# Products first, into all four accumulators: the order of work inside a seven-product matrix multiplication

## The chip, the core and the metric

The kernel runs on one core of one Trainium2 chip. The metric is device time in microseconds (us) of one execution, lower is better. TensorE is called PE below, VectorE DVE, ScalarE ACT, GpSimd POOL and the queue of SyncE SP, as in the profile.

## The reference, cut

One layer of a decoder for 256 tokens of width 2048, all in float32:

```python
h = rmsnorm(x, attn_norm)
gq, gk, gv, gr, ga1, sq, sk, sv, mq, gates = split(h @ w_in)     # one combined projection
y_gla = (rmsnorm(gated_linear_attention(gq, gk, gv, ga1)) * silu(gr)) @ w_br_gla
y_sb  = stick_breaking_attention(rmsnorm(sq), rmsnorm(sk), sv) @ w_br_sb
y_mem = softmax_attention(rmsnorm(mq), memory_k, memory_v) @ w_br_mem
g = sigmoid(gates.reshape(256, 3, 2048))
x = x + (g[:, 0] * y_gla + g[:, 1] * y_sb + g[:, 2] * y_mem) @ w_o
h2 = rmsnorm(x, ffn_norm)
gate, up = split(h2 @ w_gate_up)                                 # 2 x 5632 columns
x = x + (silu(gate) * up) @ w_down
```

The weights (2048 x 13328, 2048 x 11264, 5632 x 2048 and smaller ones) are streamed from HBM once. Every product keeps float32 precision: each operand is split into a high and a low part, and three matmuls (high x high, high x low, low x high) make one product of a 128-row chunk.

## The kernel before, in words

**Splitting a weight.** A load (SP queue, 1 MB) brings four 128-row chunks of a 512-column weight block into a tile `raw`. `half` takes two of these chunks: ACT copies them to `wh` (line 151, the rounded high part), DVE subtracts to get `wl` (line 152). One such pair of chunks is called a *half* below. The `wh`/`wl` tiles form a ring of 6 pairs (5 in the stages from the gates to `w_o`), and ACT can write a pair only after PE has finished with the half that used it 6 (or 5) halves earlier. The four engines have in-order queues of their own; a scheduler of the framework sets the order in each queue when the program is built.

**`sgemm`** multiplies the 256 tokens by two 512-column blocks (j = 0, 1) at once. It has four accumulators in PSUM, `o[t, j]` (t is the half of the tokens, 128 each; named `acc` in the profile), and two more PSUM tiles, `x0` and `x1` (named `tmp`). Over the first 2p of the K chunks it does not multiply out the 2 x 2 blocks with eight products but with seven, in the manner of Winograd and Strassen: p1 to p7, with sums of tokens prepared beforehand (`forms`: `sh`, `sl`, `sd` in the profile) and sums of weights made on the way. The other chunks are multiplied in the ordinary way by `rest`, whose half feeds two accumulators (12 matmuls); a half of a product feeds one (6 matmuls). The weight tiles are `q[21]`, `q[22]`, `q[11]`, `q[12]` (row of chunks, then column block).

- p1 (`a`) makes a product in `x0` and copies it to `o[0, 0]` (ACT, line 314, in `put`).
- p5 (`g`) adds `q[22]` to `q[21]` (DVE, line 283), makes a product in `x1` and copies it to an SBUF piece `c["p5"]` (ACT, line 345).
- p6 (`h`) adds `q[12]` to `q[21]` (DVE), makes a product in `x0`; DVE writes p5 - p6 to `o[0, 1]` (line 316). It also issues the POOL DMA `q[22] += q[12]` (line 351).
- p2 (`b`) and p3 (`e`) accumulate in `o[0, 0]` and `o[0, 1]`. p2 issues the POOL DMA `q[11] += q[21]` (line 331), except in `w_down`, where DVE does this sum.
- p7 (`i`) makes a product of the new `q[22]` in `x0` and gives it to `o[1, 0]` and, as p5 - p7, to `o[1, 1]`. Before the change both go to SBUF pieces `c[1, 0]` (ACT) and `c[1, 1]` (DVE), and `result` adds each to its accumulator at the end (DVE, line 404).
- q4 (`f`) accumulates a product of the new `q[11]` in `o[1, 0]`.

The list `seq` sets the order in which these steps are written down. There are three: `late` (the first group of `w_o` and of the FFN), `end` (the last group) and the ordinary one. A group is one call of `sgemm`; 28 of the 31 groups use the ordinary order: six of `w_in`, six of the gates, one of `w_o`, ten of `w_gate_up`, five of `w_down`. In these p is 4, so a product is two halves (12 matmuls), the lists `l21`, `l22`, `l11`, `l12` are empty, and `r0` and `r1` (the ordinary chunks for j = 0 and j = 1) have four halves each, two in the last part of `w_down`. `step()` between halves advances background work (other stages' transposes, attention, making of forms).

The caller receives j = 0 and j = 1 as soon as their accumulators are complete and turns them into sigmoids, SiLUs or copies.

Of the kernel before, what the change touches and what calls it, by code (L numbers as in the profile page):

```python
# [77 lines left out]
def trunk(ctx: ExitStack, tc: tile.TileContext, a, out):  # L78
# [37 lines left out]
    def acc():  # L116
        return ps.tile([P, NB], F32, tag="acc", name="acc", bufs=4)
# [7 lines left out]
    def step():  # L125
        while background:
            try:
                return next(background[0])
            except StopIteration:
                background.pop(0)  # L130
# [57 lines left out]
    def piece():  # L188

        if kit is not None:  # L190
            return kit.tile([P, NB], F32, tag="cv", name="cv", bufs=8)
        if not halves:
            two = gog.tile([P, 2, NB], F32, name="two", tag="g_og")
            halves.extend([two[:, 1], two[:, 0]])
        return halves.pop()

    def gemm(xs, w, c0, row0=0, first=(), load=nc.sync.dma_start, fine=False):

        o = [acc() for _ in range(2)]
        nk = len(xs)
        sizes = list(first)
        sizes += [min(KG, nk - k) for k in range(sum(sizes), nk, KG)]
        k0 = 0
        for n in sizes:
            xp = [x() if callable(x) else x for x in xs[k0 : k0 + n]]
            raw, done = loads()  # L210
            r0 = row0 + k0
            load(raw[:, :n], w[c0 // NB, :, r0 : r0 + n])
            for g in range(0, n, 2):
                m = min(2, n - g)
                wh, wl = (x[:].rearrange("p (k n) -> p k n", k=2) for x in parts())
                split(wh[:, :m], wl[:, :m], raw[:, g : g + m])
                if g + m == n:
                    done()
                for t in range(2):
                    s = slice(t * P, (t + 1) * P)  # L220
                    for j in range(m):
                        xh, xl = xp[g + j]
                        k = k0 + g + j
                        pe.matmul(o[t][:], xh[:, s], wh[:, j], start=k == 0, stop=False)  # L224
                        pe.matmul(o[t][:], xh[:, s], wl[:, j], start=False, stop=False)  # L225
                        pe.matmul(o[t][:], xl[:, s], wh[:, j], start=False, stop=k == nk - 1)  # L226
                    if fine and t == 0:
                        step()
                step()
            k0 += n  # L230
        return o

    def sgemm(xs, forms, w, blks, p, row0=0, late=False, moved=True, base=None, end=False):
# [21 lines left out]
        o = {(t, j): acc() for t in range(2) for j in range(2)}  # L255
        x0, x1 = tmp(), tmp()
        c, q, loaded, begun = {}, {}, {}, set()
# [7 lines left out]
        def mm(dst, xp, wh, wl, last):  # L265

            xh, xl = xp
            pe.matmul(dst[:], xh, wh, start=id(dst) not in begun, stop=False, skip_group_check=True)  # L268
            begun.add(id(dst))
            pe.matmul(dst[:], xh, wl, start=False, stop=False, skip_group_check=True)  # L270
            pe.matmul(dst[:], xl, wh, start=False, stop=last, skip_group_check=True)  # L271

        def half(raw, g):
            wh, wl = (x[:].rearrange("p (k n) -> p k n", k=2) for x in parts())
            split(wh, wl, raw[:, g : g + 2])
            return wh, wl

        def prod(dst, left, b, last, *sums):

            for g in range(0, p, 2):  # L280
                for to, of in sums:
                    x, y = (q[i][0][:, g : g + 2] for i in (to, of))
                    dve.tensor_tensor(x, x, y, op=ALU.add)  # L283
                wh, wl = half(q[b][0], g)
                for i in range(2):
                    mm(dst, left[g + i], wh[:, i], wl[:, i], last and g + i == p - 1)
                step()
# [4 lines left out]
        def formed(f):  # L292
            return [[x[:, f, i] for x in forms] for i in range(SP)]
# [5 lines left out]
        def put(at, *src):  # L299

            if base and at[0]:
                v = base(at[1])
                dve.tensor_tensor(v, v, src[0][:], op=ALU.add)
                if len(src) > 1:
                    dve.tensor_tensor(v, v, src[1][:], op=ALU.subtract)
                return
            if late or at[0]:
                c[at] = piece()
                dst = c[at][:]
            else:  # L310
                dst = o[at][:]
                begun.add(id(o[at]))
            if len(src) == 1:
                act.copy(dst, src[0][:])  # L314
            else:
                dve.tensor_tensor(dst, src[0][:], src[1][:], op=ALU.subtract)

        def fetch(i, j, k):
            q[i] = load(j, k)
            loaded.update({(j, k + g): (q[i][0], g, None) for g in range(p, SP, 2)})  # L320

        def p1():
            fetch(21, 0, SP)
            prod(x0, single(1, 0), 21, False)
            put((0, 0), x0)
# [18 lines left out]
            c["p5"] = piece()  # L344
            act.copy(c["p5"][:], x1[:])

        def p6():

            if 12 not in q:
                fetch(12, 1, 0)  # L350
            nc.gpsimd.dma_start(q[22][0][:, :p], q[12][0][:, :p], accum_op=ALU.add)
            prod(x0, formed(2), 21, False, (21, 12))
            put((0, 1), c["p5"], x0)

        def p7():
            prod(x0, formed(3), 22, True)
            put((1, 0), x0)
            put((1, 1), c["p5"], x0)

        def rest(j, k, last):  # L360
# [14 lines left out]
        r0, r1 = ([(rest, j, k) for k in range(2 * SP, nk, 2)] for j in range(2))  # L375

        l21, l22, l11, l12 = (
            [(rest, j, k + g) for g in range(p, SP, 2)] for j, k in ((0, SP), (1, SP), (0, 0), (1, 0))
        )
        a, b, e, f, g, h, i = ((x,) for x in (p1, p2, p3, q4, p5, p6, p7))  # L380
        if late:
            seq = [a, *l21, b, *l11, *r0, *r1[:1], (made,), g, *l22, *r1[1:2], h, e, *l12, *r1[2:3], i, f, *r1[3:]]
        elif end:
            seq = [a, *l21, *r0, g, h, *l22, b, *l11, e, *l12, i, f, *r1]
        else:
            seq = [a, *l21, *r0[:2], g, *r0[2:], h, *l22, b, *l11, e, *l12, *r1[:2], i, *r1[2:3], f, *r1[3:]]
        uses = {21: [a, g, h, f, *l21], 22: [g, h, i, *l22], 11: [b, f, *l11], 12: [h, e, *l12]}
        into = {p2: [(0, 0)], p3: [(0, 1)], q4: [(1, 0)]}
        todo = [into.get(x[0], [(t, x[1]) for t in range(2)] if len(x) > 1 else []) for x in seq]
# [159 lines left out]
    gain, i = {}, 0  # L549
# [52 lines left out]
    o = gemm(mems, w_kv, 0, first=(1, 1, 2))  # L602
# [40 lines left out]
    def ra():  # L643
        return ring("ra", 4)
# [85 lines left out]
    def wide(dst, c0, p=SP):  # L730
        for j, result in sgemm(xs, sx, w_in, (c0 // NB, c0 // NB + 1), p):
            for t in range(2):
                v = dst[:, t, j * NB : (j + 1) * NB]
                act.activation(v, result(t), AF.Copy, scale=r_x[:, t : t + 1])
# [89 lines left out]
    for j, result in sgemm(xs, sx, w_in, (O_GR // NB, O_GR // NB + 1), SP):  # L824
        for t in range(2):
            sg, o = ra()[:], result(t)
            sigmoid(sg, o, t, False)
            v = gr[:, t, j * NB : (j + 1) * NB]
            act.activation(v, o, AF.Copy, scale=r_x[:, t : t + 1])
            dve.tensor_tensor(v, v, sg, op=ALU.mult)  # L830
# [177 lines left out]
    def pairs(t):  # L1008
        return [(t[0][:, k], t[1][:, k]) for k in range(8)]
# [5 lines left out]
    for n in range(0, D, NB):  # L1015
        o = gemm(pairs(o_mem), a["w_br_mem"], n, fine=True)
# [7 lines left out]
    for n in range(0, D, NB):  # L1024
# [8 lines left out]
        o = gemm(pairs(o_sb), a["w_br_sb"], n, fine=True)  # L1033
# [8 lines left out]
    for b in (2, 1, 0):  # L1042
# [3 lines left out]
        for n0 in range(0, D, 2 * NB):  # L1046
# [7 lines left out]
            for j, result in sgemm(xs, sx, a["w_gate"], (k, k + 1), 4):  # L1054
                gs.append([piece()[:] for t in range(2)])
                for t in range(2):
                    g = gs[-1][t]
                    act.activation(g, result(t), AF.Sigmoid, scale=r_x[:, t : t + 1])
                    m = merged[:, t, n0 + j * NB : n0 + (j + 1) * NB]
                    if b == 2:  # L1060
                        dve.tensor_tensor(m, m, g, op=ALU.mult)
                    elif b == 1:
                        dve.tensor_tensor(g, yr[j][:, t], g, op=ALU.mult)
                        dve.tensor_tensor(m, m, g, op=ALU.add)
# [60 lines left out]
    for part in (range(0, 4), range(4, 8), range(8, NF)):  # L1125
        fs, tiles = [], []
        for i in part:
            for j, result in sgemm(hs, sf, a["w_gate_up"], (i, NF + i), 4 if i else 2, late=i == 0):
                if j == 0:
                    g = [piece()[:] for t in range(2)]  # L1130
# [6 lines left out]
            f = [kit.tile([P, 4, T], F32R, name=f"f{x}", bufs=4) for x in "hl"]  # L1137
# [83 lines left out]
```

## Time and profile before

| what | us |
|---|---|
| median of three runs | 1613.08 (1612.8 to 1614.85) |
| the profiled execution | 1612.68 |
| its span, first to last instruction | 1610.9 |
| PE busy (matmuls) | 1603.4, 100% of the span |
| DVE busy | 1356.4, 84% |
| ACT busy | 1044.8, 65% |

The profiled execution ran at the full granted PE clock (1.000). A busy PE row counts overlapping matmuls: one takes 390 ns from start to end, but the next starts about 227 ns after it, so the distance between starts, and not the busy share, tells whether PE loses time.

### The profile page before, as it was taken

The numbers are of one execution on the slowest core, as the hardware profiler recorded it, in microseconds if no ns is written. First come the engines' busy times: TensorE is split into PE (matmuls) and PEld (weight loads), VectorE is DVE, ScalarE is ACT, GpSimd is POOL, SyncE is SP. The second block draws the span as 40 slices with busy tenths as digits, with TensorE's granted clock in tenths as the row PEclk, the third lists the DMA queues.
The fourth block names the chain that finished last, engine by engine and source line by source line (L and its number), as shares of the span: only waits on it lengthen the run. The fifth ranks groups of instructions, "written<-read, shape, count | busy, mean of one in ns | idle before, by whom it ended". The sixth has DMA issues, their size and how long they took to land.

```text
span 1610.9 us, 19440 instructions
## 1 busy us (share of the span) xinstructions
PE 1603.4 (100%) x7220; PEld 1317.3 (82%) x7220; DVE 1356.4 (84%) x1545; ACT 1044.8 (65%) x1274; POOL 73.0 (5%) x95
## 2 busy tenths in 40 slices
PE   9999999999999999999999999999999999999999
PEld 6888888888888888788888888888888888888887
DVE  6777788897776788897799998988888989888997
ACT  7665677776755666665666757666666666666663
POOL 0000000000000000000000000000110000110000
PEclk9999999999999999999999999999999999999999
DMA  9775768667656888887757868777897687897684
GB/s 378 290 262 171 236 215 260 213 174 254 209 186 206 262 264 262 271 280 287 230 192 257 267 239 254 247 259 239 261 281 252 214 262 242 259 276 244 200 327 125
DMA packets 66175, 395.04 MB, mean 245 GB/s; under 512 B 7296, under 2 KB 13952, under 8 KB 21024
## 3 DMA queue, kind: packets, MB, share of 16 engines
q1 hardware_dynamic: 51344, 324.36, 52.5%
q0 software_dynamic: 11792, 66.59, 21.7%
q10 hardware_dynamic: 2944, 2.85, 0.6%
q8 instruction: 56, 0.92, 0.2%
q14 instruction: 39, 0.32, 0.1%
HBM read 325.09 MB, written 12.58 MB: 210 GB/s over the span
## 4 chain that ended last, share of the span: by engine, by line
PE 98%; DMA 1%; DVE 0%; ACT 0%; issue 0%; SPq 0%; DVEq 0%; ACTq 0%
PE acc L268 19%; PE acc L271 19%; PE acc L270 19%; PE tmp L268 7%; PE tmp L270 7%; PE tmp L271 7%; PE acc L225 5%; PE acc L224 5%; PE acc L226 5%; PE tmp L455 2%; DMA raw<-in_w_mem_kv 0%; PE tmp L693 0%; PE tmp L721 0%; PE tmp L803 0%; DMA xraw<-in_memT 0%; PE tmp L786 0%
## 5 line engine op out<-in xcount | busy, mean ns | idle before, releaser
L152 DVE TENSOR_TENSOR wl<-raw,wh 128x1024 fp32r<-128x1024 f32 (+1 forms) x767 | 922.0, 1222 | 212.5 <-ACT wh L151 199.6
L151 ACT CAST wh<-raw 128x1024 fp32r<-128x1024 f32 (+1 forms) x767 | 798.8, 1052 | 434.5 <-PE acc L271 224.5
L268 PE MATMUL acc<-wh,xTh 128*128 128x512 f32 x480 | 190.4, 397 | 0.0
L270 PE MATMUL acc<-wl,xTh 128*128 128x512 f32 x480 | 187.2, 390 | 0.0
L271 PE MATMUL acc<-wh,xTl 128*128 128x512 f32 x480 | 186.9, 390 | 0.0
L268 PE MATMUL acc<-wh,hh 128*128 128x512 f32 x452 | 178.9, 396 | 0.0
L270 PE MATMUL acc<-wl,hh 128*128 128x512 f32 x452 | 176.1, 390 | 0.0
L271 PE MATMUL acc<-wh,hl 128*128 128x512 f32 x452 | 175.1, 390 | 0.0
L283 DVE TENSOR_TENSOR raw<-raw 128x1024 f32<-128x1024 f32 x133 | 161.4, 1221 | 0.6
L224 PE MATMUL acc<-wh,oh 128*128 128x512 f32 x320 | 126.7, 397 | 0.6 <-ACT wh L151 0.6
L225 PE MATMUL acc<-wl,oh 128*128 128x512 f32 x320 | 125.5, 392 | 1.1 <-DVE wl L152 1.1
L226 PE MATMUL acc<-wh,ol 128*128 128x512 f32 x320 | 124.9, 390 | 0.0
L268 PE MATMUL tmp<-wh,sh 128*128 128x512 f32 x294 | 115.9, 394 | 0.7 <-ACT wh L151 0.7
L271 PE MATMUL tmp<-wh,sl 128*128 128x512 f32 x294 | 114.8, 390 | 0.0
L270 PE MATMUL tmp<-wl,sh 128*128 128x512 f32 x294 | 114.6, 390 | 0.0
L268 PEld LDWEIGHTS acc<-wh,xTh 128*128 128x128 f32 x480 | 90.1, 188 | 20.8 <-ACT acc L314 3.1
L271 PEld LDWEIGHTS acc<-wh,xTl 128*128 128x128 f32 x480 | 90.1, 188 | 19.1
L270 PEld LDWEIGHTS acc<-wl,xTh 128*128 128x128 f32 x480 | 90.2, 188 | 17.7
L268 PEld LDWEIGHTS acc<-wh,hh 128*128 128x128 f32 x452 | 84.9, 188 | 18.7 <-ACT acc L314 1.0
L271 PEld LDWEIGHTS acc<-wh,hl 128*128 128x128 f32 x452 | 84.8, 188 | 18.0
L270 PEld LDWEIGHTS acc<-wl,hh 128*128 128x128 f32 x452 | 84.9, 188 | 16.7
L268 PE MATMUL acc<-wh,fh 128*128 128x512 f32 x220 | 86.5, 394 | 0.0
(312 smaller groups left out, 2333.8 us busy)
## 6 DMA issues: line engine op xcount, KB each, us to landing
raw<-in_w_gate_up SPq DMA_DIRECT2D x88, 1024.0 KB, 6.0
raw<-in_w_in SPq DMA_DIRECT2D x56, 1024.0 KB, 5.7
raw<-raw POOLq DMA_DIRECT2D x52, 1024.0 KB, 8.0
raw<-in_w_gate SPq DMA_DIRECT2D x48, 1024.0 KB, 7.5
raw<-in_w_down SPq DMA_DIRECT2D x44, 1024.0 KB, 7.2
raw<-in_w_o SPq DMA_DIRECT2D x16, 1024.0 KB, 5.0
raw<-in_w_mem_kv SPq DMA_DIRECT2D x15, 1024.0 KB, 10.5
raw<-in_w_br_mem SPq DMA_DIRECT2D x8, 1024.0 KB, 5.0
```

The costliest lines, as they stand in the source:

```text
L151: act.copy(hi, src)
L152: dve.tensor_tensor(lo, src, hi.bitcast(F32), op=ALU.subtract)
L224: pe.matmul(o[t][:], xh[:, s], wh[:, j], start=k == 0, stop=False)
L225: pe.matmul(o[t][:], xh[:, s], wl[:, j], start=False, stop=False)
L226: pe.matmul(o[t][:], xl[:, s], wh[:, j], start=False, stop=k == nk - 1)
L268: pe.matmul(dst[:], xh, wh, start=id(dst) not in begun, stop=False, skip_group_check=True)
L270: pe.matmul(dst[:], xh, wl, start=False, stop=False, skip_group_check=True)
L271: pe.matmul(dst[:], xl, wh, start=False, stop=last, skip_group_check=True)
L283: dve.tensor_tensor(x, x, y, op=ALU.add)
L455: pe.transpose(dst, src, ident)
```

## The change

In the ordinary order the six products p1, p5, p6, p2, p3, p7 now come first, then two halves of `r0`, then the product q4, the other halves of `r0`, and `r1` last. p7's results are written into the accumulators `o[1, 0]` and `o[1, 1]` directly, since nothing has been accumulated there yet, and so `result` has nothing to add. The DMA `q[22] += q[12]`, with the load of `q[12]` that it needs, is written at the end of p5, not at the start of p6. The `late` and `end` orders stay.

```diff
@@ put
-            if late or at[0]:
+            if late or id(o[at]) in begun:
                 c[at] = piece()
@@ p5, p6
             c["p5"] = piece()
             act.copy(c["p5"][:], x1[:])
 
-        def p6():
-
             if 12 not in q:
                 fetch(12, 1, 0)
             nc.gpsimd.dma_start(q[22][0][:, :p], q[12][0][:, :p], accum_op=ALU.add)
+
+        def p6():
+
             prod(x0, formed(2), 21, False, (21, 12))
@@ the ordinary order
-            seq = [a, *l21, *r0[:2], g, *r0[2:], h, *l22, b, *l11, e, *l12, *r1[:2], i, *r1[2:3], f, *r1[3:]]
+            seq = [a, g, h, b, e, i, *r0[:2], f, *r0[2:], *l11, *l12, *l21, *l22, *r1]
```

After the change the lines of the file behind p6 stand one lower; line 351 becomes 349. Three places show what the scheduler makes of it, all in the fourth group of the gates (the second of `b == 1`). First PE, at the end of p1; before, with `x0` = tmp_5635, `x1` = tmp_5636 and the accumulators acc_5631 (t = 0, j = 0) and acc_5633 (t = 1, j = 0):

```order
L268 MATMUL tmp_5635<-wh_5649,xTh_319 128x512
L270 MATMUL tmp_5635<-wl_5650,xTh_319 128x512
L271 MATMUL tmp_5635<-wh_5649,xTl_320 128x512
L268 MATMUL tmp_5636<-wh_5697,sh_944 128x512
L268 MATMUL acc_5633<-wh_5662,xTh_319 128x512
L270 MATMUL acc_5633<-wl_5663,xTh_319 128x512
L271 MATMUL acc_5633<-wh_5662,xTl_320 128x512
L268 MATMUL acc_5631<-wh_5662,xTh_319 128x512
```

And now, with `x0` = tmp_5605 and `x1` = tmp_5606:

```order
L268 MATMUL tmp_5605<-wh_5619,xTh_319 128x512
L270 MATMUL tmp_5605<-wl_5620,xTh_319 128x512
L271 MATMUL tmp_5605<-wh_5619,xTl_320 128x512
L268 MATMUL tmp_5606<-wh_5633,sh_944 128x512
L270 MATMUL tmp_5606<-wl_5634,sh_944 128x512
L271 MATMUL tmp_5606<-wh_5633,sl_945 128x512
```

Before, matmuls into the accumulator that ACT fills from p1 followed p1 almost at once; now p5 and p6 stand between.

Second, ACT around q4's splits (raw_5780, now raw_5682, is `q[11]`; raw_5694, now raw_5630, is `q[22]`). Before:

```order
L151 CAST wh_5857<-raw_5694 128x1024
L151 CAST wh_5867<-raw_5694 128x1024
L151 CAST wh_5883<-raw_5881 128x1024
L151 CAST wh_5899<-raw_5780 128x1024
L151 CAST wh_5909<-raw_5780 128x1024
L151 CAST wh_5928<-raw_5881 128x1024
L314 COPY cv_5877<-tmp_5635 128x512
```

And now:

```order
L151 CAST wh_5725<-raw_5630 128x1024
L151 CAST wh_5735<-raw_5630 128x1024
L151 CAST wh_5749<-raw_5747 128x1024
L151 CAST wh_5765<-raw_5747 128x1024
L151 CAST wh_5781<-raw_5682 128x1024
L151 CAST wh_5791<-raw_5682 128x1024
L314 COPY acc_5603<-tmp_5605 128x512
```

p7's copy stands behind q4's two splits in both orders; before, it went to an SBUF piece (`cv`), now it goes to the accumulator `o[1, 0]` (acc_5603), which the half of raw_5747 needs.

Third, DVE at the start of the same group (raw_5607 is `q[21]`, raw_5656 `q[12]`, raw_5682 `q[11]`; L1064 and L1065 belong to the results of the group before). Now:

```order
L152 TENSOR_TENSOR wl_5645<-raw_5607,wh_5644 128x1024
L1064 TENSOR_TENSOR cv_5589<-yr_5277,cv_5589 128x512
L283 TENSOR_TENSOR raw_5607<-raw_5607,raw_5656 128x1024
L1065 TENSOR_TENSOR merged_3758<-merged_3758,cv_5589 128x512
L1064 TENSOR_TENSOR cv_5590<-yr_5277,cv_5590 128x512
L152 TENSOR_TENSOR wl_5661<-raw_5607,wh_5660 128x1024
L1065 TENSOR_TENSOR merged_3758<-merged_3758,cv_5590 128x512
L152 TENSOR_TENSOR wl_5672<-raw_5607,wh_5671 128x1024
L152 TENSOR_TENSOR wl_5685<-raw_5682,wh_5684 128x1024
L152 TENSOR_TENSOR wl_5695<-raw_5682,wh_5694 128x1024
```

Before, at the same place:

```order
L404 TENSOR_TENSOR cv_5553<-acc_5308,cv_5553 128x512
L152 TENSOR_TENSOR wl_5679<-raw_5660,wh_5678 128x1024
L1063 TENSOR_TENSOR cv_5619<-yr_5303,cv_5619 128x512
L152 TENSOR_TENSOR wl_5698<-raw_5637,wh_5697 128x1024
L1064 TENSOR_TENSOR merged_3776<-merged_3776,cv_5619 128x512
L283 TENSOR_TENSOR raw_5637<-raw_5637,raw_5694 128x1024
```

The adds of line 404 are gone, and the splits behind the old group's results are now those of p6 and p2 and not those of an ordinary half.

## The prediction

> **What bounds the kernel now.** I read the page first: the busy shares and the chain that ended last.
>
> ```profile
> PE 1603.4 (100%) x7220; PEld 1317.3 (82%) x7220; DVE 1356.4 (84%) x1545; ACT 1044.8 (65%) x1274; POOL 73.0 (5%) x95
> PE 98%; DMA 1%; DVE 0%; ACT 0%; issue 0%; SPq 0%; DVEq 0%; ACTq 0%
> ```
>
> PE carries 98% of the chain. The busy share counts overlap, so the pace comes from PE's timeline where nothing disturbs it; these are the first and the last of 29 matmuls.
>
> ```profile
> 599.62 0.39 PE L270 MATMUL acc<-wl,xTh 128*128 128x512 f32 x1
> ...
> 605.97 0.39 PE L271 MATMUL acc<-wh,xTl 128*128 128x512 f32 x1
> ```
>
> 28 intervals take 6.35 us: 0.227 us for each matmul, 1.36 us for a half of a product (6 matmuls), 2.72 us for a half of `rest` (12). The change leaves the number of matmuls as it is, so it can only win where PE waits now and only lose where it makes PE wait. Next, what PE waits for: the row of p1's copy (line 314) with its waiters, and the list of waits.
>
> ```profile
> L314 ACT COPY acc<-tmp x29: 570/570/587, 145.1 to 1576.6; 128x512 f32<-128x512 f32 x29
>   PEld acc L268: 5.4, 17
> PE tmp L268 <- ACT wh L151: 0.7, 1, 0.7
> ACT wh L151 <- DMA raw<-raw: 9.0, 6, 2.2
> ```
>
> PE's weight loads wait 17 times for ACT's copy, 5.4 us together. One 0.7 us wait for a split lies in the gates. The last row is no wait of PE: ACT waits six times for the sums that POOL's DMAs make in `q[22]` and `q[11]`, 2.2 us at the most, and PE has enough halves in hand to cover it.
>
> **The change, part by part.** Times below count from p1's first matmul in a group.
>
> *The wait after p1.* Before, matmuls into `o[0, 0]` follow p1 after one product half or less, while ACT drains p1. Now p5 and p6 (24 matmuls, 5.4 us) stand between, and the copy lasts 0.57 us. All of the 5.4 us of wait goes: -5.4. What is late next is p6's subtraction into `o[0, 1]`, which p3 needs one product (2.7 us) later; it costs nothing.
>
> *The stall in the fourth group of the gates.* The chain shows it:
>
> ```profile
> 666.26 0.69 DVE cv L1063
> ...
> 668.01 0.69 DVE merged L1064
> 668.69 0.48 DVE raw L283
> ...
> 669.75 1.22 DVE wl L152
> 670.97 1.15 DVE raw L283
> 672.21 1.06 ACT wh L151
> 673.31 0.50 PE tmp L268
> ```
>
> DVE is late with the results of the group before when p6's sum becomes due right behind `r0`. In the new order p5 and its sum come first there, and DVE is relieved of the group's two adds of line 404 (1.2 us, next row): -0.7.
>
> *The adds of line 404.*
>
> ```profile
> L404 DVE TENSOR_TENSOR cv<-acc,cv x50: 682/685/694, 578.0 to 1544.6; 128x512 f32<-128x512 f32 x50
> L404 DVE TENSOR_TENSOR two<-acc,two x12: 683/685/691, 192.7 to 426.3; 128x512 f32<-128x512 f32 x12
> 662.01 1.29 DVE L1063 TENSOR_TENSOR cv<-yr,cv 128x512 f32<-128x512 f32 x2
> ```
>
> Two adds of this shape back to back take 1.29 us and one takes 0.69, so each occupies DVE for 0.60. Of 62 adds, two a group, 8 stay in the new program (the `late` and `end` groups and one more); 54 x 0.60 = 32 us leave DVE. In the time I count nothing for it, since PE sets the end; it is slack.
>
> *The dense part.* The six products now stand side by side: 72 matmuls, 16.3 us of PE, in place of products mixed with `r0` and `r1`. What DVE must do for them:
>
> ```profile
> 1012.89 2.35 DVE L283 TENSOR_TENSOR raw<-raw 128x1024 f32<-128x1024 f32 x2
> 1029.25 9.18 DVE L152 TENSOR_TENSOR wl<-raw,wh 128x1024 fp32r<-128x1024 f32 x8
> ```
>
> Eight subtractions take 9.18 us, so 1.14 each; two sums 2.35, so 1.13 each. Twelve subtractions, four sums and p6's write come to 12 x 1.14 + 4 x 1.13 + 0.6 = 18.8 us, 2.5 more than PE's 16.3. This would starve PE if DVE started level with it. It starts ahead: in `r1` a half lasts PE 2.72 us and DVE 1.14, so DVE fills the ring (five or six halves) before p1 begins and owes only the last six or seven of the twelve. The window of the ordinary group (in the gates) and of the worst one (one that also makes forms, in `w_gate_up`) show the average room:
>
> ```profile
> 621.20:662.20 41.00, 41.00 (x182) 33.81 (x181) 35.28 (x35) 26.90 (x29) 1.71 (x2) 1.00 0.81 257
> 1007.00:1049.00 42.00, 42.00 (x190) 34.71 (x190) 40.95 (x45) 26.63 (x32) 0.86 (x1) 1.00 0.74 255
> ```
>
> The columns are sum of the stretch, then busy us of PE, weight loads, DVE, ACT, POOL; then clock, DMA share, GB/s. DVE is busy 35.3 of 41.0 us in the first and 41.0 of 42.0 in the second. For the three groups that make forms I take +0.3 us each where `r0` begins, and +1 for the group of `w_o`, which no row shows in this order: +2. The bounds: 0 if the two adds less in each of these groups are enough; 2.5 us in every one of the 28 groups, 70 us, if DVE never got ahead, which the ring excludes.
>
> *p7's copy and the DMA into q[11].* This is the new wait. p7's product ends at 16.3 us, and the first half of `r0` writes `o[0, 0]` (1.36 us) and then `o[1, 0]`, at 17.7. ACT must have copied p7 there by then. ACT's queue holds q4's two splits ahead of that copy, and these wait for the DMA `q[11] += q[21]` (line 331), which POOL issues behind DVE's second split of p2. Before, the copy went to a piece that nobody needed soon. The rows for the sum are ACT's pace, the sigmoid, and the DMA's time to landing in all 52 cases, in the gates and `w_o` (line 331), and in `w_in` (331, then line 351):
>
> ```profile
> 717.91 3.98 ACT L151 CAST wh<-raw 128x1024 fp32r<-128x1024 f32 x4
> L1058 ACT ACTIVATE cv<-acc,r_x 128x512 f32<-128x512 f32 x10 | 6.8, 680 | 0.0
> raw<-raw POOLq DMA_DIRECT2D x52, 1024.0 KB, 8.0
> DMA to landing us min/median/max: 7.8/8.0/9.3
> DMA to landing us min/median/max: 6.9/7.3/8.2
> DMA to landing us min/median/max: 7.1/8.8/10.6
> ```
>
> Four casts take 3.98 us with the last one's full 1.05, so 0.97 each. In the second and third groups of the gates DVE turns to the last group's results when their sigmoid ends (0.2 + 0.7 = 0.9 us), then two multiplications, p6's sum and four subtractions: 0.9 + 2 x 0.60 + 1.13 + 4 x 1.14 = 7.8. Landing 8.0 later: 15.8. Two casts (1.94) and the copy (0.57) end at 18.3; with 0.1 for the handing over, 18.4 against 17.7: 0.7 us of wait in each. In the fourth and fifth each result costs two DVE operations, 1.2 more: 9.0, 17.0, 19.6: 1.9 each. The sixth has no such operation; I take 0.2. Sum 2 x 0.7 + 2 x 1.9 + 0.2 = 5.4. In the FFN the results need one DVE operation or none ahead of the sums and the ring holds six: the DMA goes out at about 6.3 and lands at about 13.9 at the pace of `w_gate_up`,
>
> ```profile
> DMA to landing us min/median/max: 7.5/7.6/8.1
> 1048.44 0.49 PE L455 MATMUL tmp<-cst,cv 128*128 128x128 f32 x3
> ```
>
> but a third cast of `r0` stands ahead of the copy, which ends at about 13.9 + 3 x 0.97 + 0.57 = 17.4. Background transposes on PE (three in 0.49 us less the 0.2 of drain, about 0.1 each, some eight a group) push the need to about 18.6. That leaves 1.2 us, so no wait. In `w_down` DVE makes this sum and no DMA stands there. In `w_in` the DMA is the quickest: nothing. The price lies between 0 (landing after 6.9, the fastest row: 14.7 and 17.3 in the second group, no wait; the fourth still waits 0.8) and 1.3 us more in each of five gates groups and 0.1 to 0.5 in ten FFN groups, with landing after 9.3; 10.6 was seen only for the other DMA. I take 8.0, the median of the very stage.
>
> **The sum.** 1612.7 (the profiled execution) - 5.4 - 0.7 + 2.0 + 5.4 = 1614.0; the median stands 0.4 above the profiled execution: 1614.4, rounded to 1614.5. A wait found and a wait lost of the same size, in the same PE queue.
>
> **The rivals.** *No new wait.* The copy is in time if the DMA lands by 17.7 - 0.1 - 1.94 - 0.57 = 15.1, that is 0.7 us sooner than I count in the second and third groups and 1.9 sooner in the fourth and fifth: by a landing near the 6.9 us of `w_in`'s fastest, or by a DVE that reaches p2's second split that much earlier. Then 1612.7 - 6.1 + 0 to 1 = 1607, faster. For it speaks that the six waits of ACT for such a DMA now are 1.5 us on average and none reaches PE; against it, that the copy now has 1.4 us of cover (one half into `o[0, 0]`) and no longer the rest of the group. [...]
>
> *The DMA lands late everywhere.* The new order asks for loads in another rhythm, and the gates' windows show 81% DMA share. If landing goes to 9.3, the row's maximum, the gates' five groups lose 1.3 us more each (6.5), the FFN's ten about 0.5 (5): 1614.5 + 11.5 = 1626, slower. It decides once landing comes 1.2 us later than in the row, where the FFN's margin is gone.
>
> *The dense part starves PE in `w_in`.* There attention's chains of small operations sit in the queues of DVE and ACT, between the splits, and a half may come late although the average has room. DVE's deficit of 2.5 us, less a cover of one half, gives 1 to 2 us in five groups: +7.5, 1622, slower. Against it: PE's present waits for splits are single cases of 0.7 us or less.
>
> **How the numbers follow.** Forecast as summed 0.46 (1610 to 1617 by itself); no new wait 0.22 (1607); late DMA 0.17 (1626); dense part 0.15 (1622). 0.2%, about what a measurement of this kernel can tell, is 3.2 us: the same from 1609.9 to 1616.3. Of the forecast's 0.46 I put 0.36 in that band, 0.05 below, 0.05 above; of no new wait 0.20 below; the two slower rivals give 0.30 above and 0.02 within. Faster 0.25, same 0.40, slower 0.35. The range goes from the first rival to the third, 1606 to 1628; less than 2 in 10 lies outside.
>
> **What the profile after would show.** Line 314's copy into `acc` should count 56, not 29, and its waiters should move from p1's copy to p7's, 0.7 to 1.9 us each, about 17.7 us behind p1 in the second to fifth groups of the gates. The adds (then line 405) count 8, and DVE's busy time falls by about 32 us plus the overlap. ACT's wait for `raw<-raw` grows beyond 9.0 us. If PE waits for splits (wh, wl) of p3, p7 or `r0`, the dense part was mis-sized; if PE waits for ACT's copy in the FFN also, the landing was. The forecast is wrong if the copy is not behind the casts in time, or if a load for the next group, asked for in the new rhythm, comes late to p1, which no term here holds.

## The result, and the profile after

| | before | after |
|---|---|---|
| median of four runs, us | 1613.30 | 1640.97 (1640.36 to 1641.40) |
| ratio | | 1.017, interval 1.0158 to 1.0182 |
| profiled span, us | 1610.9 | 1638.9 |
| granted PE clock, mean | 1.000 | 0.998 |

The change makes the kernel 1.7% slower. The forecast of 1614.5 and its upper end of 1628 were both too low. The page after, busy times:

```profile
PE 1611.1 (98%) x7220; PEld 1318.6 (80%) x7220; DVE 1332.9 (81%) x1491; ACT 1037.3 (63%) x1274; POOL 72.9 (4%) x95
```

DVE has 54 instructions less and is busy 23.5 us less; PE, which sets the end, is the one that lost. The list of waits of the matmuls, of after, longest in total first (us together, times, longest):

```profile
PE acc L268 <- ACT acc L314: 13.8, 8, 3.4
PE acc L224 <- ACT wh L151: 1.8, 1, 1.8
PE tmp L268 <- ACT wh L151: 1.6, 1, 1.6
PE tmp L583 <- DVE zeros L580: 1.2, 1, 1.2
PE tmp L456 <- DVE hl L155: 1.2, 2, 0.7
```

The row that heads it did not exist before: eight matmuls into an accumulator wait for ACT's copy at line 314, up to 3.4 us. One of these places, in the second group of `w_o`, in the rows of PE (p1's first matmul), POOL, ACT and the DMA (start, duration, and in brackets the idle time before and what ended it):

```profile
884.36 0.39 PE L268 MATMUL tmp<-wh,oh 128*128 128x512 f32 x1
901.70 0.87 POOL L331 DMA_DIRECT2D raw<-raw  x1 [10.97 <-DVE wl L152]
DMA to landing us min/median/max: 9.0/9.0/9.0
904.52 1.05 ACT L151 CAST wh<-raw 128x1024 fp32r<-128x1024 f32 x1 [0.30 <-PE acc L271]
910.77 1.99 ACT L151 CAST wh<-raw 128x1024 fp32r<-128x1024 f32 x2 [5.20 <-DMA raw<-raw]
912.67 0.58 ACT L314 COPY acc<-tmp 128x512 f32<-128x512 f32 x1
```

POOL issues `q[11] += q[21]` as soon as DVE has made p2's second split. It lands 9.0 us later; ACT stands idle for 5.2 us in front of q4's first cast, makes both casts, and only then copies p7's product, which PE had finished at 908.4 (its first matmul at 905.68 and 12 x 0.227). The matmul that needs the copy came 3.5 us late.

Where the 28 us lie is read by laying the two traces side by side: both have 7220 matmuls and transposes on PE in the same stages, so the start of the k-th after, less the start of the k-th before, says how far the kernel had fallen behind there. Taken at the first matmul of a group's p1, where the orders meet again, in us gained (-) or lost (+) since the mark before (the sums are rounded):

| kernel | start, memory stage | `w_in`, attention | gates 1 to 3 | gates 4 to 6 | `w_o`, late FFN group | first ordinary FFN group | second ordinary FFN group | rest of the FFN | sum |
|---|---|---|---|---|---|---|---|---|---|
| after | +1.2 | +4.6 | 0.0 | +4.2 | +10.8 | +6.0 | +0.6 | +0.6 | +28.0 |
| pieces | +0.4 | +3.8 | -0.5 | -0.6 | +6.2 | +0.9 | +1.4 | -0.2 | +11.5 |
| sum_dve | +0.1 | -0.3 | -0.5 | -0.8 | +7.1 | +0.9 | +2.0 | +4.0 | +12.5 |
| q4_last | +1.6 | -0.1 | -0.5 | -1.7 | +7.1 | +5.1 | +0.5 | -0.5 | +11.5 |
| p7_before_p3 | +1.5 | +6.4 | -0.5 | -1.7 | +12.4 | +0.8 | +0.9 | -0.1 | +19.8 |
| q4_last_old2 | 0.0 | -0.2 | -0.5 | -1.7 | 0.0 | 0.0 | +5.5 | -0.7 | +2.4 |
| q4_last_no_step | +1.4 | -0.1 | -0.5 | -1.7 | +3.0 | +1.8 | +0.5 | -0.6 | +3.9 |
| p5_ahead | +0.1 | -0.8 | +0.7 | +9.2 | +0.6 | -0.2 | -0.1 | -2.0 | +7.6 |
| dma_early | +0.1 | -0.1 | 0.0 | 0.0 | 0.0 | 0.0 | 0.0 | -0.4 | -0.5 |
| mix | +1.0 | -0.2 | -0.4 | -1.7 | 0.0 | +1.6 | +0.5 | -1.0 | -0.4 |
| mix_r1 | +0.3 | +6.9 | -0.5 | +1.1 | 0.0 | +0.1 | +1.6 | +18.5 | +28.0 |

The first row says it: some 17 of the 28 us are lost in two groups, the second of `w_o` and the first ordinary one of the FFN, 4.6 in `w_in` and attention, 4.2 in the last gates. In the fourteen ordinary FFN groups behind them and the last one the two orders run nearly level (+1.2 in all). The other rows are the experiments below. The first column is the same instructions in all kernels; its spread of 0.0 to 1.6 us goes with how late the first loads land (ACT waited 2.06 us for one of `in_memT` after and 0.67 before; PE waited at line 224 for splits of the first weights 0.6 us before, 1.8 after, and 2.2 to 2.4 in the three kernels with +1.4 to +1.6), and it is no effect of an edit.

### The profile page after: what moved, and what is told of

It is laid out like the page before. It is cut to its first block, busy times and chain, and to the rows that moved or that the text cites. A ratio compares the mean times of both kernels' runs of the same rounds, so it can differ in the third digit from the quotient of the medians.

```text
span 1638.9 us, 19421 instructions
## 1 busy us (share of the span) xinstructions
PE 1611.1 (98%) x7220; PEld 1318.6 (80%) x7220; DVE 1332.9 (81%) x1491; ACT 1037.3 (63%) x1274; POOL 72.9 (4%) x95
## 5 line engine op out<-in xcount | busy, mean ns | idle before, releaser
L283 DVE TENSOR_TENSOR raw<-raw 128x1024 f32<-128x1024 f32 x133 | 162.8, 1224 | 3.5
L268 PEld LDWEIGHTS acc<-wh,xTh 128*128 128x128 f32 x480 | 90.2, 188 | 28.6 <-ACT acc L314 10.8
```

## The experiments

Two theories stood against each other. *Queue*: ACT's copy of p7 is late because it stands behind casts that wait for a DMA. *Density*: six products in a row ask more of DVE than it has, and the copy is only where that shows first. Times below are medians; a ratio is against the kernel before on the same chip.

**pieces: the copy is no longer waited for.**

```
@@ put
-            if late or id(o[at]) in begun:
+            if late or at[0]:
```

> The new order, but p7's two results go to SBUF pieces again and are added at the end (54 adds of DVE back). Queue theory: PE waited 13.8 us for ACT's copy of p7 into o[1,0], because the copy stands in ACT's queue behind q4's two casts and these wait for the DMA into q[11]; the gaps there are 15.1 us, and two stretches at half clock behind the two longest cost about 3 us more. With pieces no matmul waits for this copy: 1641 - 15 - 3 = 1623 (1620 to 1626), what is left being the stalls in the second group of w_o, w_in and at the start. Rival, density: six products in a row need more of DVE than there is, the copy is only where it shows first, and PE waits for q4's splits instead: 1632 to 1641.

Measured 1625.2 us, 1.0076 (1.0061 to 1.0091). Some 16 us of the 28 are gone, and the row for line 314 is no longer in the list of waits. ACT still stands idle for the DMA, even longer:

```profile
ACT wh L151 <- DMA raw<-raw: 51.4, 19, 5.4
```

In the changed kernel it was 44.3 us in 17 waits. So that idling costs PE nothing unless something PE wants soon stands behind it. What stays is 6.2 us in `w_o`, 3.8 in `w_in` and 2.3 in the first two ordinary FFN groups.

**sum_dve: the DMA is gone.** DVE makes the sum in `q[11]`.

```
@@ sgemm
-        nk = len(xs)
+        nk, moved = len(xs), moved and end
```

> The new order, but DVE makes the sum in q[11] in all ordinary groups, so no DMA stands between p2 and q4. Queue theory, if it is the DMA's time to landing that makes ACT's queue late: the wait for p7's copy goes in the gates, w_in and the first ordinary FFN group, and two sums of 1.13 us more on DVE cost nothing or 1 us in each group that makes forms: 1622 to 1628. Density theory: more work for DVE in the dense part, so as slow as now or slower: 1641 to 1655.

Measured 1625.5 us, 1.0077 (1.0061 to 1.0094). The waits of the matmuls for the copy shrink to 0.3 us in two places; `w_in` and the gates are now 0.3 and 1.3 us faster than before. In `w_o` 7.1 of 10.8 us stay, so these are not the copy's. The extra sums show in the FFN behind its first ordinary group: +6.0, in three steps of about 2 us in the groups that also make forms, where DVE had next to no time left (busy 40.95 of 42.00 us in such a group before).

**q4_last: q4's casts are behind the copy.**

```
-            seq = [a, g, h, b, e, i, *r0[:2], f, *r0[2:], *l11, *l12, *l21, *l22, *r1]
+            seq = [a, g, h, b, e, i, *r0, f, *l11, *l12, *l21, *l22, *r1]
```

> The new order, but q4 comes behind all four halves of r0, so p7's copy stands in ACT's queue ahead of q4's casts (behind two casts of r0 that wait only for PE). Queue theory: every wait for p7's copy is gone but for some 0.3 us where the last cast of r0 waits for the ring; the DMA has 5.4 us more: 1623 (1619 to 1626). Density theory: the stalls move to r0's splits, 1632 to 1641.

Measured 1622.07 us, 1.0058 (1.0043 to 1.0073), the best of these four. In `w_in` and the gates all that the change lost is gone. The one copy that still holds PE, for 2.4 us, is in the first ordinary FFN group. There ACT can run further ahead, and one cast of q4 still stands ahead of the copy:

```profile
988.29 1.04 ACT L151 CAST wh<-raw 128x1024 fp32r<-128x1024 f32 x1 [3.48 <-DMA raw<-raw]
989.24 0.58 ACT L314 COPY acc<-tmp 128x512 f32<-128x512 f32 x1
```

**p7_before_p3: the copy ahead, by moving the product.**

```
-            seq = [a, g, h, b, e, i, *r0[:2], f, *r0[2:], *l11, *l12, *l21, *l22, *r1]
+            seq = [a, g, h, b, i, e, *r0[:2], f, *r0[2:], *l11, *l12, *l21, *l22, *r1]
```

> The new order, but p7 comes before p3, so its copy stands ahead of q4's two casts in ACT's queue and a whole product lies between p7's end and the need for o[1,0]; the DMA into q[11] is as it was. The DMA into q[22] has 2.7 us less. Queue theory: the waits for the copy are gone, 1623 (1619 to 1627); what could come instead is ACT's wait for the DMA into q[22] ahead of p7's splits, up to 1 us in each gates group. Density theory: unchanged, 1632 to 1641.

Measured 1630.7 us, 1.0110 (1.0095 to 1.0125), a miss by 4 us at the upper end. The copy is on time (no matmul waits for it; the last three groups of the gates gain 1.7 us). But `q[22] += q[12]` now has a product less, and in `w_o`, where DVE is late with the sums in front of it, p7's own cast waits for it, and PE with it:

```profile
895.29 1.04 ACT L151 CAST wh<-raw 128x1024 fp32r<-128x1024 f32 x1 [4.55 <-DMA raw<-raw]
PE tmp L268 <- ACT wh L151: 6.1, 1, 6.1
```

I had allowed for this with up to 1 us in the gates; it came in another place, six times as long, and 10.2 us at half clock (894.13 to 904.37; the mean granted clock of this run is 0.996) go with it. `w_in` loses 6.4 us here, more than in the changed kernel; 3.6 of them are two waits of attention's transposes for DVE (1.9 and 1.7), which come up again below.

**q4_last_old2 and q4_last_no_step: the two bad groups.** With the queue mended, the second group of `w_o` still loses 7 us. DVE's rows at the start of that group, of after, out of more than 20 us without a pause:

```profile
882.86 1.28 DVE L405 TENSOR_TENSOR cv<-acc,cv 128x512 f32<-128x512 f32 x2
884.06 1.29 DVE L1103 TENSOR_TENSOR x<-cv,xr 128x512 f32<-128x512 f32 x2
...
887.59 0.48 DVE L155 SCALAR_TENSOR_TENSOR hl<-tmp,vecs,hh 128x256 fp32r<-128x256 f32 x1
887.99 1.22 DVE L283 TENSOR_TENSOR raw<-raw 128x1024 f32<-128x1024 f32 x1
889.36 0.88 DVE L155 SCALAR_TENSOR_TENSOR hl<-tmp,vecs,hh 128x256 fp32r<-128x256 f32 x2
890.15 1.22 DVE L283 TENSOR_TENSOR raw<-raw 128x1024 f32<-128x1024 f32 x1
```

p1 began at 884.4. The group before this one has the `late` order and hands its results over in one lump at the end (L405, L1103), the background prepares the next stage's input (L155), and the dense products want their sums (L283) and splits at the same time. The second experiment gives both bad groups (`old` is set for the second group of `w_o` and the first ordinary one of the FFN) their old order back:

```
@@ q4_last_old2 (on q4_last)
+            if old:
+                seq = [a, *l21, *r0[:2], g, *r0[2:], h, *l22, b, *l11, e, *l12, *r1[:2], i, *r1[2:3], f, *r1[3:]]
```

> q4 behind r0 as in q4_last, but the second group of w_o and the first ordinary group of the FFN keep the order of before. Theory: what q4_last still loses is 7.0 us in that group of w_o and 4.8 in that group of the FFN, where DVE still has the results of the late group and the chunks of the next stage's input to make while the six products want four sums and twelve splits; elsewhere the dense order costs nothing. So 1622 - 11.8 = 1610 to 1613, level with before or up to 0.2% faster. Rival: the dense order loses wherever it stands and the stalls move to the next group: 1617 or more.

Measured 1616.02 us, 1.0015 (1.0006 to 1.0024): between the theory's 1613 and the rival's 1617. In `w_o` the loss is exactly gone (0.0), and in the first ordinary FFN group too. But there it moved instead of going: the dense group that now follows the old-order group makes forms as well and inherits its late results, 5.5 us. The next one keeps the new order and takes the background steps out of the products of these two groups (`quiet`):

```
@@ q4_last_no_step (on q4_last), prod
-                step()
+                if not quiet:
+                    step()
```

> q4 behind r0 as in q4_last, but in those two groups no background work is advanced between the halves of products, so that the transposes and DVE's eight small operations for the next input (line 155, 0.4 us each) fall behind the products' first sums. If the background is what makes DVE late: of the 7.0 us in w_o about 2 to 4 stay, of the 4.8 in the FFN 2 to 4, total 1616 to 1619. If the results of the late group (three adds of line 405 and four of the residual, 4.2 us) and the sums alone are too much: 1620 to 1622.

Measured 1616.09 us, 1.0015 (1.0006 to 1.0024). Of the 7.1 us in `w_o` 3.0 stay, of the 5.1 in the FFN group 1.8. So more than half of what these groups lose goes when the background work leaves the products. With it go the two stretches at half clock that q4_last has there (1.2 and 1.4 us; the mean granted clock is 0.997 there and 0.999 here) and 0.9 us of the FFN group's wait for the copy (2.4, now 1.5). That the rest in `w_o` is the late results and the sums themselves fits DVE's rows; no run isolates it.

**p5_ahead and dma_early: parts of the change alone, on the kernel before.** The first tests the forecast's largest gain, PE's wait for p1's copy; the second is the moved DMA `q[22] += q[12]` of the diff without the rest.

```
@@ p5_ahead
-            seq = [a, *l21, *r0[:2], g, *r0[2:], h, *l22, b, *l11, e, *l12, *r1[:2], i, *r1[2:3], f, *r1[3:]]
+            seq = [a, *l21, g, *r0, h, *l22, b, *l11, e, *l12, *r1[:2], i, *r1[2:3], f, *r1[3:]]
```

> The kernel before with one move: p5 comes straight behind p1, ahead of r0, so the first matmul into o[0,0] comes two halves later. This removes the 17 waits of the weight loads for p1's copy (5.4 us). The prediction's theory, that this wait was PE's: 5.4 us faster than before, 0.9966. The other theory, that a weight load runs ahead of its matmul and the wait was hidden (no wait of matmuls for that copy is in the list): 0.3 us or less, ratio 0.9995 to 1.0005.

> The kernel before with the DMA q[22] += q[12] and its load at the end of p5 and nothing else: the DMA goes out two halves earlier. Both theories: no effect, within 1 us (ratio 0.9995 to 1.0006), since p7 comes some 20 us later in that order; a loss of several us would mean that part of the 28 us comes from this DMA or from the load of q[12] that now stands earlier in SP's queue.

p5_ahead measured 1620.35 us, 1.0045 (1.0032 to 1.0058), a miss for both theories: slower. The weight loads' wait is gone, as it was meant to be (who waited for line 314, in this kernel):

```profile
  PEld acc L268: 0.4, 1
```

It was 5.4 us in 17 waits before. But the matmuls gained less, some 3 to 3.5 us: the intervals between their starts around the ends of the 29 copies (up to 0.9 us behind each) held about 4.8 us beyond the undisturbed 0.229 before, and 1.3 to 1.8 here, by which intervals are counted. In the FFN, where nothing else differs, the gain is 2.3 us in the fifteen ordinary groups and the last one. Against it stand 9.4 us lost in the fourth and fifth group of the gates (4.9 and 4.5), where p5's sum and splits now come while DVE is still busy with the results of the group before:

```profile
665.11 1.21 DVE L283 TENSOR_TENSOR raw<-raw 128x1024 f32<-128x1024 f32 x1
666.35 0.69 DVE L1063 TENSOR_TENSOR cv<-yr,cv 128x512 f32<-128x512 f32 x1
666.96 1.22 DVE L283 TENSOR_TENSOR raw<-raw 128x1024 f32<-128x1024 f32 x1
```

About 4 of the 9.4 us are not waits but half clock behind them: 13 and 8 intervals between matmuls of some 0.427 us in place of 0.227, in these windows (the clock is the third number from the end):

```profile
669.28:676.10 6.82, 6.13 (x14) 4.78 (x15) 6.82 (x7) 3.44 (x5) 0.00 (x0) 0.50 1.03 249
717.07:720.48 3.41, 3.41 (x9) 2.64 (x9) 3.41 (x4) 0.66 (x2) 0.00 (x0) 0.50 1.09 249
```

The new order does not have this loss in the gates. A result of j = 0 comes half a group earlier there and needs no add of line 404, which would explain it; no run isolates it. dma_early measured 1613.3 us, 0.9999 (0.9989 to 1.0008): the moved DMA by itself does nothing, as expected.

**mix and mix_r1: put together.** mix is q4_last with the old order in the second group of `w_o` and without background steps in the products of the first ordinary FFN group. mix_r1 moves q4 one half further:

```
@@ mix_r1 (on mix)
-            seq = [a, g, h, b, e, i, *r0, f, *l11, *l12, *l21, *l22, *r1]
+            seq = [a, g, h, b, e, i, *r0, *l11, *l12, *l21, *l22, *r1[:1], f, *r1[1:]]
```

> q4 behind r0; the second group of w_o in the order of before (the FFN's first ordinary group in the new one), and no background step between the halves of products in the FFN's first ordinary group. By the pieces seen apart: before, minus 2.4 us up to the end of w_o, plus 2.3 in that FFN group, minus 0.6 behind it: 0.7 us faster than before, ratio 0.9990 to 1.0005. Rival, the stalls move on to the group behind whatever is mended: ratio 1.0015 as in the two halves of this mixture.

> As mix, but q4 comes behind the first half of r1, so that no cast of q4 stands ahead of p7's copy in the FFN either, whose ring lets ACT run one half further ahead; there q4's first cast still held the copy for 1.5 us. Queue theory: 1.5 us less than mix in that group, no wait for the copy left anywhere: ratio 0.9980 to 0.9998. Rival: j = 0 is complete one half and one product later, so its results come closer to the end and DVE starts the next group late again: the same as mix or up to 5 us slower.

mix measured 1611.76 us, 0.9990 (0.9981 to 0.9999): 1.8 us faster than before, at the edge of what can be told: level with the kernel before, if not a little faster, and without the loss of the changed one. mix_r1 measured 1639.12 us, 1.0161 (1.0148 to 1.0175), as slow as the change itself, far beyond either expectation. Its rows show the first theory's mechanism with another transfer:

```profile
PE acc L268 <- ACT acc L315: 15.0, 10, 3.4
...
1075.25 1.04 ACT L151 CAST wh<-raw 128x1024 fp32r<-128x1024 f32 x1 [4.77 <-DMA raw<-in_w_gate_up]
1076.20 0.58 ACT L315 COPY acc<-tmp 128x512 f32<-128x512 f32 x1
```

(L315 is the copy's line here.) Now ACT waits for a load from HBM ahead of the copy, 27.8 us in ten waits for that matrix against 7.8 in four in mix, and 12.0 and 10.7 us for the matrices of the gates and `w_in`, for which ACT does not wait at all in mix. `q[11]` is kept until 80% of a group's matmuls are done instead of 73%; that the late release of its tile is what makes the load late fits, but no run isolates it.

## Why the prediction was wrong, step by step

**The mechanism of the loss was right, its places were not.** The last term of the sum, p7's copy behind q4's two casts behind the DMA, is what happened, and pieces, sum_dve and q4_last each remove it in another way. In the gates it was even sized well:

| group of the gates | DMA issued behind p1's start: forecast, measured | wait: forecast, measured |
|---|---|---|
| second | 7.8, 7.25 | 0.7, 0 |
| third | 7.8, 7.23 | 0.7, 0.15 |
| fourth | 9.0, 8.35 | 1.9, 1.24 |
| fifth | 9.0, 8.34 | 1.9, 1.28 |
| sixth | -, 9.73 | 0.2, 2.96 |
| sum | | 5.4, 5.6 |

The landing, 8.0 us in the forecast, was 8.0 in the median of the six groups of the gates. DVE was half a microsecond earlier than I counted, and the sixth group, which I let off with 0.2 because its own results cost no DVE operation, was the worst: DVE had the attention stage's `ol` tiles and two late results of another stage in its queue ahead of p2. The sum agreed because two errors cancelled.

**The step that failed is the FFN's and `w_o`'s part of that term.** The prediction takes one time for the whole FFN, the DMA going out 6.3 us behind p1's start, which leaves a margin of 1.2 us; `w_o` has no part in this term at all (its one microsecond stands under the dense part). For nine of the ten ordinary groups of `w_gate_up` that time was right: 6.1 to 6.8 us, and no matmul waits there. The two groups that follow a `late` group are not in their stride: DVE begins them with a backlog, and p2's second split, which lets the DMA go, comes late. In `w_o` POOL issued it 17.3 us behind p1 (884.36 and 901.70 in the rows above), in the FFN 12.1:

```profile
982.23 0.39 PE L268 MATMUL tmp<-wh,hh 128*128 128x512 f32 x1
994.33 0.88 POOL L331 DMA_DIRECT2D raw<-raw  x1 [15.04 <-DVE wl L152]
```

There the copy came 3.5 and 3.4 us late, 7 us in place of 0. `w_in`, set to nothing because its landing was the quickest before (7.3 in the median), had three waits for it of 0.8 to 1.0 us: its DMAs went out 6.1 to 10.2 us behind p1 and landed after 8.1.

**The dense part was mis-sized.** +2 in the sum; q4_last, where hardly a copy is waited for, still loses 7.1 us in `w_o` and, its 2.4 us of copy taken off, 2.7 in the FFN group (in both some 1.3 us of it half clock, of which below). The average room in a group's window (35 of 41 us) told nothing of the group that starts with 7 us of other work in DVE's queue. In `w_in` the rival of the starved dense part has a share too, by a longer way: where ACT waits for the DMA, DVE's next split waits for ACT, and attention's operations behind that split in DVE's queue reach PE's transposes late. pieces, which keeps ACT's waits, has these two rows, and sum_dve and q4_last, which remove most of them, do not:

```profile
PE tmp L456 <- DVE mq L524: 1.8, 1, 1.8
PE tmp L456 <- DVE sk L524: 1.7, 1, 1.7
```

**The gain of 5.4 us was 3 to 3.5.** It was a wait of the weight loads, and I booked it as PE's. p5_ahead removes 5.0 us of that wait and wins some 3 to 3.5, so part of it cost the matmuls nothing. The changed kernel's trace shows where such a part can lie: a weight load (0.19 us) starts some 0.22 us ahead of its matmul, while the matmul before it still runs (908.18 and 908.40 behind p7's product), and at the copy that held PE longest the load's row has 3.80 us of wait and the matmul's 3.37. That fits these 1.5 to 2 us; no run isolates it. In ACT's queue nothing ran ahead: the copy of p7 stood behind both of q4's casts and their 5.20 us of waiting, 4.3 us after its product had ended.

**The stall in the fourth group of the gates** (-0.7) went as forecast: q4_last gains 1.2 us there. **The adds** count 8 and line 314's copies into an accumulator 56, as forecast; DVE's busy time fell by 23.5 us and not 32 (why is open), and none of it can be seen in the time, which rose.

**The rivals.** "DMA lands late everywhere" named the right direction (1626) for a wrong reason: the landing stayed at 8.0 in the median in the gates, and was 7.9 for 7.6 before in `w_gate_up` and 8.1 for 7.3 in `w_in`, short of the 1.2 us more that this rival asks for; where most was lost it was the issue that came late.

**What no term held: the clock.** Behind the two longest waits PE ran at half speed for a while. The windows (us; busy times; then the granted clock) around the first:

```profile
900.00:909.60 9.60, 9.60 (x44) 7.81 (x42) 7.67 (x8) 4.49 (x5) 0.87 (x1) 1.00 0.70 130
909.60:913.10 3.50, 0.33 (x2) 0.00 (x0) 1.25 (x2) 2.33 (x3) 0.00 (x0) 1.00 1.00 417
913.10:918.00 4.90, 4.70 (x14) 3.71 (x15) 4.07 (x4) 2.17 (x3) 0.00 (x0) 0.65 1.01 426
918.00:927.00 9.00, 9.00 (x41) 7.47 (x40) 4.83 (x5) 4.21 (x4) 0.00 (x0) 1.00 0.98 392
```

Seven intervals of 0.427 us in place of 0.227 there, and seven behind the wait in the FFN group: 2.8 us together.

So of the 28.0 us: the waits for p7's copy 15.1 (by the gaps between matmuls at eight places), the half clock 2.8, the start 1.2; the other 9 are DVE's lateness in `w_o` (about 5, by the gaps between matmuls within 15 us of p1's start), the late transposes in `w_in` (2), and some 2 us of small stalls, net of the gains, that I have not taken apart. The copy's share is shown by three edits that remove it each in another way; the shares of the rest are read from gaps.

## What to carry to other kernels

A copy out of an accumulator that is wanted soon must not stand in an engine's queue behind work that waits for a transfer (15.1 us here); a buffer between them (the SBUF pieces, here) or a later place for the waiting work is worth more than the adds that it costs an engine with slack (54 adds of 0.60 us on DVE here, for some 16 of the 28 us). When an order is made denser, cost it in the group that starts with the largest backlog on the helping engine, not in the average one. And a wait in the weight loads' row told more than PE lost here (5.0 us against some 3 to 3.5): take it as an upper bound.

## What the runs showed of the hardware

PE's waits of 3.5 and 3.4 us in `w_o` and in the FFN were each followed, 4.6 and 4.7 us after their beginning, by 3.41 us at half the granted clock, from 914.39 and from 1006.55; matmuls started 0.427 us apart there in place of 0.227. The length of one wait does not tell: behind the 2.96 us in the sixth group of the gates the clock stayed at 1.00, and in sum_dve waits of 1.6 us and less, close together, went ahead of a drop. The longer drops named above lasted two and three times 3.41 us (6.82 in p5_ahead from 669.28, 10.24 in p7_before_p3 from 894.13). Two drops of one execution began a whole multiple of 3.41 us apart: 92.16 us, 27 of them, here, and 47.79 us, 14 of them, in p5_ahead (669.28 and 717.07). The rows below are the 3.41 us ahead of the two drops here (the first with the window of the drop itself), those behind the beginning of the 2.96 us wait, which end 34 times 3.41 us before the first drop, and in sum_dve those ahead of its drop, with a window that holds it:

```profile
910.98:914.39 3.41, 1.09 (x5) 0.91 (x6) 2.54 (x3) 3.25 (x4) 0.00 (x0) 1.00 1.01 420
914.39:917.81 3.42, 3.42 (x10) 2.65 (x9) 2.78 (x3) 1.04 (x1) 0.00 (x0) 0.50 1.02 431
1003.14:1006.55 3.41, 1.26 (x5) 1.05 (x6) 2.51 (x3) 3.41 (x5) 0.00 (x0) 1.00 1.01 423
794.91:798.32 3.41, 1.67 (x7) 1.42 (x8) 3.12 (x4) 2.67 (x4) 0.00 (x0) 1.00 1.02 425
884.90:888.31 3.41, 1.68 (x5) 0.96 (x6) 3.41 (x4) 3.41 (x4) 0.00 (x0) 1.00 0.28 58
888.00:892.00 4.00, 4.00 (x12) 3.15 (x11) 4.00 (x5) 2.02 (x3) 0.00 (x0) 0.57 0.00 0
```

PE was busy for 0.32 and 0.37 of the stretches ahead of the two drops here. With the trace of the changed kernel cut into stretches of 3.41 us counted from the first drop (473 of them, from 20.1 to 1634.6 us), these two shares are the lowest; the next are 0.49 (the 1.67 us above) and 0.56, all others are 0.67 or more, and no drop came behind any of these. In sum_dve a stretch with 0.49 had one behind it. So a share of 0.49 went both ways in these runs, and no run isolates what decides.
